# First feed-forward sums moved from GpSimd to VectorE, and operand splits issued piece by piece, in a one-layer decoder trunk

## The chip, the core and the metric

One NeuronCore of a Trainium2 chip runs the whole kernel. The metric is the device time of one launch in microseconds (us), given as the median of several runs. A difference is told as a share of the time before.

## The reference

One decoder layer (DEPTH = 1) on x of 2048 tokens by 1024 features, all in float32:

```
h = rmsnorm(x);  proj = h @ w_in                    # 1024 -> 4624
ya = conformer_mixer(...);  yb = gmlp_mixer(...);  yc = mamba2_mixer(...)
x = x + concat([ya, yb, yc]) @ w_out                # 2048 -> 1024
h = rmsnorm(x)
x = x + square(relu(h @ w_ff1)) @ w_ff2             # 1024 -> 4096 -> 1024
return rmsnorm(x)
```

## The kernel before

**Precision.** TensorE (PE) works on 32-bit operands that are split: `hi` is the operand cast to the engine's rounded 32-bit type (ScalarE, ACT), `lo` is the operand less `hi` (VectorE, DVE). Every product is three matmuls, hi*hi, lo*hi and hi*lo. Each operand is therefore a load into a raw tile (issued by SyncE, SP), a cast on ACT and a subtraction on DVE before PE can use it. A cast or a subtraction of a 128x512 tile is one instruction.

**Stages.** The tokens are worked on in two halves (h = 0, 1) of 1024.

- In-projection and the three mixers, up to 1012 us.
- Out-projection: four blocks, (h, kb), where kb = 0 and 1 are the two 1024-row halves of the contraction. A block has 4 column groups nq by 4 steps c0; a step is 48 matmuls of 128x256 (`mm3`, L243 to L245). PSUM is evicted to the accumulator by DVE (L1064 for kb = 0, L1074 for kb = 1); two tiles of PSUM turn round, so an eviction may be one step late before PE waits. The weights of the next nq are loaded and split by `load_wo`/`split_w` (L231 to L233), the left sides of the next block by `load_y`/`load_split` (`hi_y`, `lo_y`), both inside a scheduling priority (`evac`) that moves their instructions ahead.
- FF1 (first feed-forward layer): each half by a seven-product scheme (Strassen-Winograd), 16 pairs j by 7 products q, two pairs taken together, so 14 steps to a group and 224 steps in all. A step is 12 matmuls of 128x512 (L988 to L990). Its left sides are w1 blocks and their sums (`sum_w1`, L970 to L975, four 128x512 operations a pair, on GpSimd, POOL), its right sides the seven x operands of that half (`load_xi`, 4 pieces each, in L946 a load, in L927/L928 the splits). Four PSUM tiles are used for products 0 to 3 and 6 and four for 4 and 5.
- After FF1's products come the squared relu on ACT and, for the second layer's right sides, sums of the results: three on POOL (L1155 to L1157) and one on DVE (L1167), all stored to DRAM (`f_d`).
- FF2: the same seven products, 12 matmuls a step, right sides `fr` split into `fahi`/`falo`, left sides `wbhi`/`wblo`.

**Prepared sums.** `prep` makes 36 items (sums of blocks of the normalized input and of the second layer's weights, `PREP`) that go back to DRAM (`t_d`, `w2t_d`): a load of two pieces into one of two buffers `pr` (L912), four 128x256 operations on POOL (L920 to L923), a store (L924). Items are taken in the last block of the out-projection, one a step, and then a few for each group of FF1. FF1's x operands of q = 1, 3, 4 and 6 are read back from `t_d`.

**Order.** The program is written as one sequence, and a scheduler orders each engine's instructions by priority; each engine then runs its own in order, waiting on semaphores. `evac` raises a priority, `behind` ties an instruction behind another without a wait. Preparation of FF1 runs ahead of its products by fixed leads, in steps (`LEADW` 7 for w1 loads, `LEADS` 5 for sums, `LEAD1` 3 for splits, `LEADX` 9 for the second half's x operands), in `ahead1`; the first seven calls of it stand after the out-projection's last block. SP issues nearly all loads from one queue; POOL issues the stores of `f_d`'s sums, ACT of the others.

Of the kernel before, what the change touches and what calls it, by code (L numbers as in the profile page):

```python
# [41 lines left out]
def kernel(  # L42
# [179 lines left out]

    def split_w(pl, src, nk, ncol, tag, name, rk, bufs=2, rbufs=2, rpl=None):
# [14 lines left out]
    def mm3(pairs, n):  # L238


        for i, outs in enumerate(pairs):
# [673 lines left out]
    def prep_sum(key, after):  # L915
# [4 lines left out]
        behind(nc.gpsimd.tensor_sub(b11, b12, b11), after)  # L920
        nc.gpsimd.tensor_sub(b12, b22, b12)
        nc.gpsimd.tensor_sub(b22, b22, b11)
        nc.gpsimd.tensor_sub(b21, b21, b22)  # L923
# [8 lines left out]
    def load_xi(h, q):  # L932

        pl, bufs = (opnd, KT * NB) if q < 4 else (xb[0], 12)
        out_ = []
        for k in range(4):
            hi = pl.tile([P, 512], F32R, tag="hi", name=f"xhi_{h}_{q}_{k}", bufs=bufs)
            lo = pl.tile([P, 512], F32R, tag="lo", name=f"xlo_{h}_{q}_{k}", bufs=bufs)
            raw = const.tile([P, 512], F32, tag="raw", name=f"xr_{h}_{q}_{k}", bufs=RAWB)
            if q in TI:  # L940
                src = t_d[h][TI[q], k * P:(k + 1) * P, :]
            else:
                kk, th = {0: (k, 0), 2: (k + 4, 0), 5: (k + 4, 1)}[q]
                src = h2_d[h][kk * P:(kk + 1) * P, th * 512:th * 512 + 512]
            with evac() if h == 0 else contextlib.nullcontext():
                nc.sync.dma_start(raw, src)  # L946
                split_to(raw, hi, lo)
            out_.append((hi, lo))
        XS[h, q] = out_
# [13 lines left out]

    def sum_w1(h, j, q):
# [3 lines left out]
        if q == 1:  # L968
            w[3], w[1] = [ffa.tile([P, 4, P], F32, tag="s", name=f"ws{i}_{h}_{j}", bufs=4) for i in range(2)]
            nc.gpsimd.tensor_add(w[3], a21, a22)  # L970
            nc.gpsimd.tensor_sub(w[1], w[3], a11)
        elif q == 4:
            nc.gpsimd.tensor_sub(a21, a11, a21)
        elif q == 5:
            last["s4"] = nc.gpsimd.tensor_sub(w[1], a12, w[1])  # L975
            w[5] = w[1]

    def split_w1(h, j, q):
        hi = ffa.tile([P, 4, P], F32R, tag="hi", name=f"w1hi_{h}_{j}_{q}", bufs=5)
        lo = ffa.tile([P, 4, P], F32R, tag="lo", name=f"w1lo_{h}_{j}_{q}", bufs=5)  # L980
        split_to(WR[h, j][q], hi, lo)
# [30 lines left out]
    for bi, (h, kb) in enumerate(blocks):  # L1012
# [67 lines left out]
        preload(1)  # L1080
        ys = ynew
    prep(sums=True)

    GRP = 2
    LEADW, LEADS, LEAD1, LEADX, LEAD2, LEADB = 7, 5, 3, 9, 3, 16
    seq1 = [(h, g * GRP + i, q) for h in range(NHALF) for g in range(NPAIR // GRP) for q in range(NP)
            for i in range(GRP)]
# [298 lines left out]
```

## Time and profile before

| | |
|---|---|
| median of 3 runs | 2720.04 us (2716.86 to 2723.82) |
| profiled execution | 2722.77 us, span 2721.0 us |
| PE busy | 2650.2 us, 97% of the span |
| DVE, ACT, POOL busy | 63%, 49%, 34% |
| mean granted clock of PE | 0.992 of full speed |

Matmuls are pipelined, so a PE that is drawn busy may still run below its rate; the count of matmuls in a stretch, against the count in an equal stretch without waits, tells what was lost. Shares of busy time of the other engines are averages over stages: POOL's work lies mostly between 1446 and 2100 us.

### The profile page before, as it was taken

The numbers are of one execution on the slowest core, as the hardware profiler recorded it, in microseconds if no ns is written. First come the engines' busy times: TensorE is split into PE (matmuls) and PEld (weight loads), VectorE is DVE, ScalarE is ACT, GpSimd is POOL, SyncE is SP. The second block draws the span as 40 slices with busy tenths as digits, with TensorE's granted clock in tenths as the row PEclk, the third lists the DMA queues.
The fourth block names the chain that finished last, engine by engine and source line by source line (L and its number), as shares of the span: only waits on it lengthen the run. The fifth ranks groups of instructions, "written<-read, shape, count | busy, mean of one in ns | idle before, by whom it ended". The sixth has DMA issues, their size and how long they took to land. (4 is left out here: it accounts for less than half of the span.)

```text
span 2721.0 us, 38968 instructions
## 1 busy us (share of the span) xinstructions
PE 2650.2 (97%) x14018; PEld 2221.0 (82%) x14018; DVE 1710.5 (63%) x2289; ACT 1327.9 (49%) x2469; POOL 915.6 (34%) x980
## 2 busy tenths in 40 slices
PE   8999999999999999999998999989999999999998
PEld 6788887778878889999997788768887888888887
DVE  6778875596997844754436766886665434545434
ACT  5547673476686343543235455555444433333332
POOL 1013243123343221213054898687896000000001
PEclk9999999999999999999999999999999999999999
DMA  3343443334343236556478666676665645555543
GB/s 119 104 130 116 148 132 94 95 116 134 117 141 119 76 115 199 186 178 214 139 248 276 203 211 203 218 240 202 207 208 193 218 147 166 190 178 178 166 120 124
DMA packets 386897, 446.80 MB, mean 164 GB/s; under 512 B 28300, under 2 KB 279920, under 8 KB 386704
## 3 DMA queue, kind: packets, MB, share of 16 engines
q1 hardware_dynamic: 335520, 314.02, 38.0%
q0 software_dynamic: 28352, 96.62, 9.6%
q10 hardware_dynamic: 22832, 33.68, 3.5%
q8 instruction: 110, 1.80, 0.3%
q14 instruction: 83, 0.68, 0.1%
HBM read 297.28 MB, written 146.93 MB: 163 GB/s over the span
## 5 line engine op out<-in xcount | busy, mean ns | idle before, releaser
L988 PE MATMUL f<-xhi,w1hi 128*128 128x512 f32 x896 | 354.6, 396 | 18.2 <-DVE u L1138 12.1
L989 PE MATMUL f<-xlo,w1hi 128*128 128x512 f32 x896 | 353.9, 395 | 1.7 <-DVE xlo L928 1.7
L988 PE MATMUL f<-wbhi,fahi 128*128 128x512 f32 x896 | 349.4, 390 | 6.2 <-ACT wbhi L927 6.2
L990 PE MATMUL f<-xhi,w1lo 128*128 128x512 f32 x896 | 353.5, 395 | 1.3 <-DVE w1lo L928 1.3
L928 DVE TENSOR_TENSOR falo<-fr,fahi 128x512 fp32r<-128x512 f32 (+1 forms) x240 | 156.9, 655 | 314.2 <-ACT fahi L927 295.7
L989 PE MATMUL f<-wblo,fahi 128*128 128x512 f32 x896 | 349.2, 390 | 0.3 <-DVE wblo L928 0.3
L990 PE MATMUL f<-wbhi,falo 128*128 128x512 f32 x896 | 349.0, 390 | 0.0
L927 ACT CAST fahi<-fr 128x512 fp32r<-128x512 f32 (+1 forms) x240 | 141.8, 592 | 371.1 <-PE f L989 362.9
L530 DVE SCALAR_TENSOR_TENSOR ca<-ht,caw,ca 128x1024 f32<-128x1024 f32 x240 | 316.1, 1317 | 5.8 <-ACT ca L526 2.6
L243 PE MATMUL mmo<-whi_o,hi_y 128*128 128x256 f32 x1024 | 297.9, 291 | 16.8 <-DVE x L1074 9.6
L245 PE MATMUL mmo<-whi_o,lo_y 128*128 128x256 f32 x1024 | 291.4, 285 | 0.0
L244 PE MATMUL mmo<-wlo_o,hi_y 128*128 128x256 f32 x1024 | 291.1, 284 | 0.0
L988 PEld LDWEIGHTS f<-xhi,w1hi 128*128 128x128 f32 x896 | 169.7, 189 | 58.4 <-issue 8.1
L243 PEld LDWEIGHTS mmo<-whi_o,hi_y 128*128 128x128 f32 x1024 | 196.1, 191 | 20.6 <-DVE x L1074 10.7
L1260 POOL TENSOR_SCALAR ss<-ss 128x1 f32<-128x1 f32 x16 | 8.4, 522 | 592.6 <-ACT junk L1256 592.6
L989 PEld LDWEIGHTS f<-xlo,w1hi 128*128 128x128 f32 x896 | 169.9, 190 | 40.4 <-DVE xlo L928 2.6
L990 PEld LDWEIGHTS f<-xhi,w1lo 128*128 128x128 f32 x896 | 169.9, 190 | 40.2 <-DVE w1lo L928 2.1
L988 PEld LDWEIGHTS f<-wbhi,fahi 128*128 128x128 f32 x896 | 168.6, 188 | 41.6 <-ACT wbhi L927 6.7
L989 PEld LDWEIGHTS f<-wblo,fahi 128*128 128x128 f32 x896 | 168.6, 188 | 35.8 <-DVE wblo L928 0.8
L244 PEld LDWEIGHTS mmo<-wlo_o,hi_y 128*128 128x128 f32 x1024 | 196.2, 192 | 1.5 <-issue 1.4
L990 PEld LDWEIGHTS f<-wbhi,falo 128*128 128x128 f32 x896 | 168.6, 188 | 34.9
L245 PEld LDWEIGHTS mmo<-whi_o,lo_y 128*128 128x128 f32 x1024 | 195.8, 191 | 0.0
(299 smaller groups left out, 6031.4 us busy)
## 6 DMA issues: line engine op xcount, KB each, us to landing
fr<-f_d SPq DMA_DIRECT2D x208, 256.0 KB, 2.7
w<-in_w_ff_dram SPq DMA_DIRECT2D x176, 256.0 KB, 2.9
f_d<-fs POOLq DMA_DIRECT2D x96, 256.0 KB, 2.7
abc<-acs_d SPq DMA_DIRECT2D x32, 512.0 KB, 4.8
raw_y<-y_d SPq DMA_DIRECT2D x64, 256.0 KB, 4.0
wraw_o<-in_w_out_dram SPq DMA_DIRECT2D x64, 256.0 KB, 4.0
pr_w<-in_w_ff_dram SPq DMA_DIRECT2D x64, 256.0 KB, 4.8
w2t_d<-pr_w POOLq DMA_DIRECT2D x32, 512.0 KB, 4.4
```

The lines of the kernel that those rows point to most:

```text
L243: nc.tensor.matmul(ps, lh, rh, start=(i == 0 and j == 0), stop=False)
L244: nc.tensor.matmul(ps, lh, rl, start=False, stop=False)
L245: nc.tensor.matmul(ps, ll, rh, start=False, stop=(i == n - 1 and j == len(outs) - 1))
L530: nc.vector.scalar_tensor_tensor(acc, ht[:, k:k + T], caw[:, k * 4 + t:k * 4 + t + 1], acc, op0=ALU.mult, op1=ALU.add)
L927: nc.scalar.copy(hi, raw)
L928: nc.vector.tensor_sub(lo, raw, hi.bitcast(F32))
L988: nc.tensor.matmul(ps, lh, rh, start=start and i == 0, stop=False, skip_group_check=True)
L989: nc.tensor.matmul(ps, lh, rl, start=False, stop=False, skip_group_check=True)
L990: nc.tensor.matmul(ps, ll, rh, start=False, stop=last, skip_group_check=True)
L1260: nc.gpsimd.tensor_scalar(s_[:, 1:2], s_[:, 1:2], s_[:, 0:1], EPS, op0=ALU.add, op1=ALU.add)
```

## The change

- The w1 sums (4 for each of 32 pairs), the three POOL sums of FF1's results (32 times) and the four operations of prepared items from the 17th on go from POOL to DVE. Prepared items 0 to 15, those of the out-projection's last block, stay on POOL. All stores stay where they are.
- The out-projection's weights are loaded and split in pieces of 256 rows, one a step: piece z + 4 is split and piece z + 6 loaded at step z. The next block's left sides (`y_step`) and FF1's right sides (`x_step`) are loaded four at a time and split one call later, two a step in FF1.
- `pin` ties each of these casts and subtractions into program order on its engine; `early` does so for the w1 sums and splits ahead of step 0.
- The seven leading calls of `ahead1` stand in the last three steps of the out-projection.
- In FF2 the first three pairs of splits are pinned, w2 ahead of f.

```diff
+    def pin(ins):
+        return tc.keep_in_program_order(ins)
...
+    def raw_split(raw, name, g=None):
+        hi, lo = hi_lo(name)
+        if g is None:
+            pin(nc.scalar.copy(hi, raw))
+            pin(nc.vector.tensor_sub(lo, raw, hi.bitcast(F32)))
...
-            prep_sum(PREP[m], after)
+            prep_sum(PREP[m], after, nc.gpsimd if m < 16 else nc.vector)
...
-        behind(nc.gpsimd.tensor_sub(b11, b12, b11), after)
-        nc.gpsimd.tensor_sub(b12, b22, b12)
...
+        behind(eng.tensor_sub(b11, b12, b11), after)
+        eng.tensor_sub(b12, b22, b12)
...
+    def x_step(h, i, n=4):
+        for m in range(i - n, i):
+            if 0 <= m < 4 * NP:
...
+                raw = xraw.pop(0)
+                pin(nc.scalar.copy(hi, raw))
+                pin(nc.vector.tensor_sub(lo, raw, hi.bitcast(F32)))
+                XS.setdefault((h, q), []).append((hi, lo))
+        for m in range(i + 4 - n, i + 4) if i else range(4):
...
+                xraw.append(raw_load(src, f"x{h}_{q}_{k}"))
...
-            nc.gpsimd.tensor_add(w[3], a21, a22)
-            nc.gpsimd.tensor_sub(w[1], w[3], a11)
+            early(nc.vector.tensor_add(w[3], a21, a22))
+            early(nc.vector.tensor_sub(w[1], w[3], a11))
...
+    def wo_load(z):
+        if z < 4 * len(wo_seq):
+            h, kb, nq = wo_seq[z // 4]
+            r0 = kb * D + z % 4 * 256
+            raw = wor[z] = wp.tile([P, 2, NQ], F32, tag="wraw", name=f"wraw_o{z}", bufs=3)
...
             for c0 in range(0, NCH, 2):
-                if nq == 3 and c0 == 4:
-                    preload(0)
+                z = 16 * bi + 4 * nq + c0 // 2
+                wo_split(z + 4)
+                wo_load(z + 6)
+                if nq == 3 and c0 > 0:
+                    y_step(c0 // 2 - 1)
...
+                if bi == len(blocks) - 1 and nq == 3 and c0 > 0:
+                    for n in {2: (-7, -6), 4: (-5, -4, -3), 6: (-2, -1)}[c0]:
+                        at[0] = n
+                        ahead1(n)
...
-            nc.gpsimd.tensor_add(s1, f21, f22)
-            nc.gpsimd.tensor_sub(s2, s1, f11)
-            st[j, "s3w"] = nc.gpsimd.tensor_sub(f21, f11, f21)
+            nc.vector.tensor_add(s1, f21, f22)
+            nc.vector.tensor_sub(s2, s1, f11)
+            st[j, "s3w"] = nc.vector.tensor_sub(f21, f11, f21)
...
+        if n < 10:
+            x_step(0, 10 + 2 * n, 2)
+        i = n - (NP * NPAIR - LEADX)
+        if i == -2 or 0 <= i < 14:
+            x_step(1, max(0, 2 * i + 2), 2)
...
-    with tc.high_priority(offset=2000):
-        for u in range(LEAD2):
+    start2 = [True]
+    for u in range(LEAD2):
+        with tc.high_priority(offset=2000):
+            load_w2(u)
             load_f(u)
-            load_w2(u)
+    start2[0] = False
```

DVE near the end of FF1's first half, before the change: `u_0_14` is an eviction that frees a PSUM tile, `xlo_*` are splits of the second half's right sides, `w1lo` of the left sides.

```order
L1167 TENSOR_TENSOR fs_0_13_16292<-f_d_13_16288,fs_0_13_16236 128x512
L928 TENSOR_TENSOR w1lo_15_2_16339<-w_0_15_01_16125,w1hi_15_2_16338 128x512
L928 TENSOR_TENSOR xlo_0_0_16404<-xr_0_0_16405,xhi_0_0_16403 128x512
L928 TENSOR_TENSOR xlo_0_1_16410<-xr_0_1_16411,xhi_0_1_16409 128x512
L928 TENSOR_TENSOR xlo_0_2_16416<-xr_0_2_16417,xhi_0_2_16415 128x512
L928 TENSOR_TENSOR w1lo_14_3_16359<-ws_0_14_16210,w1hi_14_3_16358 128x512
L928 TENSOR_TENSOR xlo_0_3_16422<-xr_0_3_16423,xhi_0_3_16421 128x512
L1138 TENSOR_TENSOR u_0_14_16355<-p_0_14_16317,f_0_14_16342 128x512
```

The same eviction and the next one on DVE after the change; `ws` are sums of w1 blocks, `pr_w` a prepared item.

```order
L939 TENSOR_TENSOR pr_w_16156<-pr_w_16156 128x256
L940 TENSOR_TENSOR pr_w_16156<-pr_w_16156 128x256
L941 TENSOR_TENSOR pr_w_16156<-pr_w_16156 128x256
L942 TENSOR_TENSOR pr_w_16156<-pr_w_16156 128x256
L1202 TENSOR_TENSOR u_0_14_16355<-p_0_14_16317,f_0_14_16342 128x512
L1013 TENSOR_TENSOR w1lo_15_3_16387<-ws_0_15_16243,w1hi_15_3_16386 128x512
L1001 TENSOR_TENSOR ws_1_0_16634<-w_1_0_10_16478,w_1_0_11_16480 128x512
L1002 TENSOR_TENSOR ws_1_0_16635<-ws_1_0_16634,w_1_0_00_16474 128x512
L1004 TENSOR_TENSOR w_1_0_10_16478<-w_1_0_00_16474,w_1_0_10_16478 128x512
L1202 TENSOR_TENSOR u_0_15_16383<-p_0_15_16336,f_0_15_16370 128x512
L1013 TENSOR_TENSOR w1lo_14_4_16408<-w_0_14_10_16102,w1hi_14_4_16407 128x512
L964 TENSOR_TENSOR xlo_0_0_16412<-raw_x_0_0_16362,xhi_0_0_16411 128x512
```

The x splits stand behind both evictions now, and sums of w1 blocks and of a prepared item have come in ahead of and between them.

SP at the end of the out-projection and the start of FF1, before: `x_d` are stores of the out-projection's result, `pr_w` loads of prepared items, `xr_1` and `xr_2` loads of the right sides of FF1's second and third product.

```order
L839 DMA x_d_66<-x_1_0_3_11836 128x2x256
L912 DMA pr_w_13516<-in_w_ff_dram 128x2x256
L946 DMA xr_1_0_13494<-t_d_8401 128x512
L946 DMA xr_1_1_13500<-t_d_8401 128x512
L912 DMA pr_w_13516<-in_w_ff_dram 128x2x256
L946 DMA xr_1_2_13506<-t_d_8401 128x512
L946 DMA xr_1_3_13512<-t_d_8401 128x512
L946 DMA xr_2_0_13676<-h_d_67 128x512
L839 DMA x_d_66<-x_1_2_3_11838 128x2x256
```

The same stretch of SP after the change, where those loads are called `raw_x_1` and `raw_x_2`.

```order
L858 DMA x_d_66<-x_1_0_3_11820 128x2x256
L931 DMA pr_w_13516<-in_w_ff_dram 128x2x256 x2
L858 DMA x_d_66<-x_1_2_3_11822 128x2x256
L256 DMA raw_x_1_0_13508<-t_d_8401 128x512
L256 DMA raw_x_1_1_13510<-t_d_8401 128x512
L256 DMA raw_x_1_2_13512<-t_d_8401 128x512
L256 DMA raw_x_1_3_13514<-t_d_8401 128x512
L931 DMA pr_w_13627<-in_w_ff_dram 128x2x256 x2
L931 DMA pr_w_13754<-in_w_ff_dram 128x2x256 x2
L858 DMA x_d_66<-x_1_4_3_11824 128x2x256
L256 DMA raw_x_2_0_13619<-h_d_67 128x512
L256 DMA raw_x_2_1_13621<-h_d_67 128x512
```

The loads of the second product's right side now stand behind a second store of the result, those of the third behind two further prepared items.

ACT at the start of FF2, before: `f_d` is the last result of FF1, `fahi` and `wbhi` are casts of FF2's right and left sides.

```order
L1110 ACTIVATE f_d_15_19510<-u_1_15_19295 128x512
L1111 ACTIVATE f_d_15_19510<-f_d_15_19510 128x512
L1129 DMA f_d_8404<-f_d_15_19510 128x512
L927 CAST fahi_0_19528<-fr_0_19526 128x512
L927 CAST fahi_0_19540<-fr_0_19538 128x512
L927 CAST fahi_0_19552<-fr_0_19550 128x512
L927 CAST fahi_0_19571<-fr_0_19569 128x512
L927 CAST wbhi_0_19534<-w_0_0_00_19532 128x512
```

The same stretch after.

```order
L1174 ACTIVATE f_d_15_19510<-u_1_15_19295 128x512
L1175 ACTIVATE f_d_15_19510<-f_d_15_19510 128x512
L1193 DMA f_d_8404<-f_d_15_19510 128x512
L1284 CAST wbhi_0_19528<-w_0_0_00_19526 128x512
L1284 CAST fahi_0_19534<-fr_0_19532 128x512
L1284 CAST wbhi_1_19540<-w_0_1_00_19538 128x512
L1284 CAST fahi_0_19546<-fr_0_19544 128x512
```

The first cast of a left side has moved from behind four casts of right sides to the place right behind FF1's last result.

## Rows read from the trace of the kernel before

**Rows 1.** The page: busy time, share and instructions of each engine.

```profile
PE 2650.2 (97%) x14018; PEld 2221.0 (82%) x14018; DVE 1710.5 (63%) x2289; ACT 1327.9 (49%) x2469; POOL 915.6 (34%) x980
```

**Rows 2.** Stretches: length, busy time (instructions) of engines, clock, DMA share, GB/s.

```profile
1012.00:1121.00 109.00, 106.17 (x891) 103.24 (x890) 59.43 (x100) 50.46 (x112) 18.64 (x18) 0.98 0.60 191
1121.00:1233.00 112.00, 111.01 (x943) 107.68 (x942) 71.84 (x145) 57.89 (x160) 24.27 (x24) 1.00 0.62 200
1233.00:1337.00 104.00, 99.67 (x827) 99.46 (x826) 43.30 (x70) 30.46 (x58) 18.53 (x18) 0.98 0.50 159
1337.00:1446.00 109.00, 100.34 (x818) 99.49 (x817) 45.79 (x95) 38.65 (x111) 50.36 (x66) 0.97 0.78 249
1446.00:1512.00 66.00, 59.24 (x253) 46.83 (x251) 43.88 (x54) 37.38 (x71) 37.43 (x42) 0.97 0.76 249
1720.00:1810.00 90.00, 76.21 (x307) 60.68 (x306) 81.07 (x76) 48.05 (x86) 64.85 (x63) 0.92 0.73 243
1810.00:2090.00 280.00, 280.00 (x1221) 228.82 (x1220) 180.26 (x187) 141.20 (x231) 221.72 (x222) 1.00 0.60 199
2090.00:2110.00 20.00, 13.51 (x51) 10.28 (x50) 11.27 (x17) 10.59 (x19) 11.16 (x14) 0.83 0.73 254
2110.00:2712.00 602.00, 602.00 (x2657) 498.64 (x2657) 279.50 (x439) 216.74 (x408) 18.16 (x28) 1.00 0.53 166
```

**Rows 3.** Waits of PE: who was waited for, us in total, times, longest.

```profile
PE f L988 <- DVE u L1138: 12.1, 4, 5.6
PE mmo L243 <- DVE x L1074: 9.6, 5, 3.6
PE mmo L243 <- DVE x L1064: 7.2, 2, 4.3
PE f L988 <- ACT wbhi L927: 6.2, 1, 6.2
```

**Rows 4.** The page's DMA issues: transfers, size, us to landing.

```profile
wraw_o<-in_w_out_dram SPq DMA_DIRECT2D x64, 256.0 KB, 4.0
```

**Rows 5.** Waits of ACT from 1012 to 1520 us.

```profile
ACT w1hi L927 <- POOL ws L971: 19.2, 2, 12.4
```

**Rows 6.** Timeline of DVE in the last block: start, duration, what, idle before.

```profile
1396.72 0.81 DVE L233 TENSOR_TENSOR wlo_o<-wraw_o,whi_o 128x512 fp32r<-128x512 f32 x1 [6.63 <-ACT whi_o L232]
```

**Rows 7.** Waits of SP's queue from 1340 to 1480 us.

```profile
SPq L912 <- DMA w2t_d<-pr_w: 24.6, 8, 7.3
SPq L912 <- DMA t_d<-pr: 17.6, 4, 6.6
```

**Rows 8.** Loads of prepared weights, 1340 to 1480 us: shortest, median, longest ns; first and last start.

```profile
L912 SPq DMA_DIRECT2D pr_w<-in_w_ff_dram x20: 539/549/1091, 1390.5 to 1457.0; - x20
```

**Rows 9.** DVE's groups in FF1, 1520 to 2090 us: busy us, mean ns, idle before.

```profile
L928 DVE TENSOR_TENSOR w1lo<-w,w1hi 128x512 fp32r<-128x512 f32 x114 | 121.8, 1071 | 11.3 <-ACT w1hi L927 11.3
L1167 DVE TENSOR_TENSOR fs<-f_d,fs 128x512 f32<-128x512 f32 x28 | 45.7, 1632 | 41.6 <-POOL fs L1156 39.0 <-issue 2.6
L928 DVE TENSOR_TENSOR xlo<-xr,xhi 128x512 fp32r<-128x512 f32 x28 | 38.6, 1397 | 3.5 <-ACT xhi L927 3.5
```

**Rows 10.** DVE's largest group in FF2, 2120 to 2700 us.

```profile
L928 DVE TENSOR_TENSOR falo<-fr,fahi 128x512 fp32r<-128x512 f32 x199 | 137.5, 691 | 286.2 <-ACT fahi L927 267.9 <-PE f L989 14.2 <-DMA xin<-x_d 2.0
```

**Rows 11.** Timeline of DVE at the end of FF1's first half.

```profile
1735.17 0.68 DVE L928 TENSOR_TENSOR w1lo<-w,w1hi 128x512 fp32r<-128x512 f32 x1
1735.78 7.67 DVE L928 TENSOR_TENSOR xlo<-xr,xhi 128x512 fp32r<-128x512 f32 x3
...
1745.99 0.68 DVE L1138 TENSOR_TENSOR u<-p,f 128x512 f32<-128x512 f32 x1
```

**Rows 12.** Waits of SP's queue in FF1, 1440 to 2100 us.

```profile
SPq L959 <- DVE w1lo L928: 317.1, 91, 9.1
```

**Rows 13.** Timeline of ACT at the start of FF2.

```profile
2098.71 2.18 ACT L927 CAST fahi<-fr 128x512 fp32r<-128x512 f32 x4 [0.40 <-ACT f_d L1111]
2100.79 2.69 ACT L927 CAST wbhi<-w 128x512 fp32r<-128x512 f32 x5
```

More of the change, by code (lines that the diff above doesn't have):

```diff
@@ L248, in mm3, with raw_load @@
                 pump()
+    def raw_load(src, name):
+        raw = const.tile([P, 512], F32, tag="raw", name=f"raw_{name}", bufs=RAWB)
+        nc.sync.dma_start(raw, src)
+        return raw
+    def raw_split(raw, name, g=None):
[3 more added lines that the diff above has]
+            pin(nc.vector.tensor_sub(lo, raw, hi.bitcast(F32)))
+        else:
+            pin(nc.scalar.activation(hi, raw, AF.Copy, scale=g))
+            pin(nc.vector.scalar_tensor_tensor(lo, raw, g, hi.bitcast(F32), op0=ALU.mult, op1=ALU.subtract))
+        return hi, lo
     def load_split(src, name, g=None):
@@ L930 @@
     XS = {}
[L932 to L949, printed above, removed]
+    xraw = []
+    def x_step(h, i, n=4):
+        for m in range(i - n, i):
+            if 0 <= m < 4 * NP:
+                q, k = m // 4, m % 4
+                pl, bufs = (opnd, KT * NB) if q < 4 else (xb[0], 12)
+                hi = pl.tile([P, 512], F32R, tag="hi", name=f"xhi_{h}_{q}_{k}", bufs=bufs)
+                lo = pl.tile([P, 512], F32R, tag="lo", name=f"xlo_{h}_{q}_{k}", bufs=bufs)
+                raw = xraw.pop(0)
[3 more added lines that the diff above has]
+        for m in range(i + 4 - n, i + 4) if i else range(4):
+            if m < 4 * NP:
+                q, k = m // 4, m % 4
+                if q in TI:
+                    src = t_d[h][TI[q], k * P:(k + 1) * P, :]
+                else:
+                    kk, th = {0: (k, 0), 2: (k + 4, 0), 5: (k + 4, 1)}[q]
+                    src = h2_d[h][kk * P:(kk + 1) * P, th * 512:th * 512 + 512]
+                xraw.append(raw_load(src, f"x{h}_{q}_{k}"))
     WR, WS = {}, {}
@@ L991, in mm3c, with ahead1, wo_split @@
             clk.pe += 3 * 227.0
-    def load_wo(h, kb, nq):
-        return [split_w((wp, wo)[q], wout[kb * D + q * 512:kb * D + (q + 1) * 512, nq * NQ:(nq + 1) * NQ], 4, NQ, "w",
-                        f"o{h}{kb}{nq}{q}", 2, 2, 3, wp) for q in range(2)]
+    GRP = 2
+    LEADW, LEADS, LEAD1, LEADX, LEAD2, LEADB = 7, 5, 3, 9, 3, 16
+    seq1 = [(h, g * GRP + i, q) for h in range(NHALF) for g in range(NPAIR // GRP) for q in range(NP)
+            for i in range(GRP)]
+    bank, st = {}, {}
+    PG = (8, 10, 11, 13)
+    xb, fwp, ps4 = [], [], []
+    def ahead1(n):
+        for lead, f in ((LEADW, load_w1), (LEADS, sum_w1), (LEAD1, split_w1)):
+            if 0 <= n + lead < len(seq1):
+                h, j, q = seq1[n + lead]
+                if f is not load_w1:
+                    f(h, j, q)
+                elif q == 0:
+                    f(h, j)
+    WO, wor = {}, {}
+    def wo_load(z):
[3 more added lines that the diff above has]
+            raw = wor[z] = wp.tile([P, 2, NQ], F32, tag="wraw", name=f"wraw_o{z}", bufs=3)
+            nc.sync.dma_start(raw, wout[r0:r0 + 256, nq * NQ:(nq + 1) * NQ].rearrange("(k p) c -> p k c", p=P))
+    def wo_split(z):
+        if z < 4 * len(wo_seq):
+            q = z % 4 // 2
+            if z % 2 == 0:
+                WO[z // 2] = [(wp, wo)[q].tile([P, 4, NQ], F32R, tag="w" + t, name=f"w{t}_o{z}", bufs=2)
+                              for t in ("hi", "lo")]
+            hi, lo = (t[:, z % 2 * 2:z % 2 * 2 + 2, :] for t in WO[z // 2])
+            raw = wor.pop(z)
+            pin(nc.scalar.copy(hi, raw))
+            pin(nc.vector.tensor_sub(lo, raw, hi.bitcast(F32)))
     ys = ynext[0]
     blocks = [(h, kb) for h in range(NHALF) for kb in range(2)]
-    wq2 = [(h, kb, nq) for h, kb in blocks for nq in range(4)]
-    wn = load_wo(*wq2.pop(0))
+    wo_seq = [(h, kb, nq) for h, kb in blocks for nq in range(4)]
+    for z in range(4):
+        with evac():
+            wo_load(z)
+            wo_split(z)
+    wo_load(4)
+    wo_load(5)
     ys[1] = load_y(0, 0, 1)
-    accs = {}
+    accs, yraw, ycur = {}, [], None
     def load_x(h, nq):
@@ L1079 @@
                     spawn(gen_n2(h, c0, nq, acc), ("n", h))
[L1080 to L1081 removed]
+        ys, ycur = ynew, y_step
     prep(sums=True)
[L1084 to L1087, printed above, removed]
[L1088 to L1104 removed]
     def ftile(nm):
@@ L1168, in ff1 @@
             store(5, s4, nc.gpsimd)
-    for n in range(-LEADW, 0):
-        ahead1(n)
+    at[0] = 0
     xbs = ctx.enter_context(ExitStack())
```

66 lines of the change are left out of this document (32 added, 34 removed).

## The prediction

> **What bounds the kernel now.** I read the page's busy shares first. PE is busy for 2650 us, 97% of the span [rows 1], so other engines' work costs only where PE waits for it, and the whole prize is what PE loses. DVE at 63% and POOL at 34% are averages; the stages have to be taken apart.
>
> The view by stretches does that [rows 2]. In it the reader is to see, for each stretch, length, PE's count and the granted clock. Two undisturbed stretches give the rates: 1810 to 2090 us has 1221 matmuls in 280.0 us, 0.2293 us each, and FF2 (2110 to 2712) 2657 in 602.0, 0.2266. For the out-projection, block 1 (1121 to 1233) has 943 in 111.0 busy, 0.1177. Length less count times rate is the loss of each other stretch, idle time and slow clock together:
>
> - block 0: 109.0 - 891 x 0.1177 = 4.1 us
> - block 1: 1.0; block 2: 104.0 - 97.3 = 6.7
> - block 3: 109.0 - 96.3 = 12.7
> - start of FF1 (1446 to 1512): 66.0 - 253 x 0.2293 = 8.0
> - middle of FF1 (1720 to 1810): 90.0 - 70.4 = 19.6, with the clock at 0.92, between the levels of 1.2 and 2.4 GHz
> - start of FF2: 20.0 - 51 x 0.2266 = 8.4
>
> Together 60.5 us. A few matmul records may be missing, so each is good to about 1 us. The list of PE's waits, third, names who was late [rows 3]: the evictions L1064 and L1074 in the out-projection, u of L1138 in FF1, the cast wbhi in FF2. So the change can bring 60 us at most, whatever else it moves.
>
> **Out-projection, blocks 0 to 2.** The evictions were late because ACT and DVE, which run in order, stood behind something not yet there. In block 2 ACT waited 12.4 us for a w1 sum of POOL that the scheduler had drawn ahead into the out-projection [rows 5]; DVE's subtractions and an eviction stood behind it. The change writes the w1 preparation into the last three steps of block 3, and the pinned splits keep their place, so this wait has nothing left to happen to: I take 7.0 of the 7.7 us of blocks 1 and 2 (bounds 0 and 7.7). In block 0 the wait on late splits goes (up to 4.1), but the first pieces of the weights now turn round in three raw tiles: the fourth load waits for the first subtraction, and a load of that kind takes 4.0 us to land [rows 4], and two splitting operations of about 0.7 follow, 5.4 us against 4.3 us (36 matmuls) that PE has before it wants that piece; their casts also stand behind the last activation of the in-projection. A new wait of about 4 takes the old one's place: I take 0, with bounds of -5.4 and +4.1.
>
> **Block 3 and the start of FF1**, 12.7 + 8.0 = 20.7 us. In block 3 DVE stood 6.63 us behind a cast whose load was late [rows 6]; that load stood on SP behind loads of prepared items, which wait up to 7.3 us until a buffer has been stored [rows 7]. Loads of out-projection pieces are issued two steps (12 us) before their split now, which covers 7.3 + 4.0. What is late next is the chain of prepared items itself. It keeps POOL, as before, and two buffers: 10 items in 1390.5 to 1457.0 us, 7.4 us each [rows 8], against 96.3/16 = 6.0 us for a step of PE without waits. Over 16 items that chain lags by some 22 us less the lead it starts with, and the loads of FF1's second and third right sides stand behind it on SP (the second of the three pairs of orders shown). So the time won in block 3 is partly waited for in FF1's first ten steps. Bounds: nothing of the 20.7 (the chain paces both), or all of it. The chain's 7.4 us holds some waiting for PE's own evictions, by x_d's stores in the same queue, which gets shorter. I take the middle, 10.7.
>
> The stretch where this falls has 0.76 of the DMA engines busy and 249 GB/s [rows 2], among the highest of the stretches shown. The Trainium skill ("DMA: Bandwidth & Descriptors", section "Issuing engines are not separate DMA queues") says that transfers of all issuing engines run on the same 16 DMA engines and interleave; by it, finer loads in another order win nothing where those engines are full, and the term would be near its lower bound, 0. The row leaves a quarter of them free, so I do not go that far.
>
> **FF1.** POOL loses 352 operations (128 w1 sums, 96 sums of results, 128 of prepared items), DVE gets them. Their first effect is on DVE's other work. A DVE subtraction with both inputs in SBUF takes 691 ns in FF2, where POOL is idle [rows 10], but 1071, 1397 and 1632 ns for the three kinds in FF1 [rows 9]; at 1735.78 three of them took 7.67 us, and the eviction u behind them came at 1745.99 [rows 11], the longest wait of PE, 5.6 us [rows 3]. With POOL's tensor work gone from FF1 but for the items of block 3, they should take what they take in FF2.
>
> The second effect is load. For a group of 14 steps, 14 x 12 x 0.2293 = 38.5 us of PE, DVE gets for each of two pairs 5 evictions, 7 splits, 1 + 3 sums of results and 4 of w1, 40 operations, and 8 halves for two prepared items. An operation behind another costs 0.61 us (1735.17 to 1735.78) [rows 11]; for a half-width one I estimate 0.4. That is 40 x 0.61 + 8 x 0.4 = 27.6 us, 72% of the group: hidden. In the 14 steps before the second half, 28 splits of x come on top, 17.1 us, in all 44.7 in 38.5: a deficit of 6.2 us, against four PSUM tiles for each set of products, of which up to three steps (8.2 us) can wait. So between 0 and 6.2 of the 19.6 us stay; I take half, 3.1, and win 16.5. If the cover is gone, all 6.2 and the clock's share with it stay, and DVE in order decides (rival C).
>
> The Trainium skill ("VectorE: DVE Perf Modes", section "The DRAIN you can't avoid") says that a DVE operation starts only when the one before has left the pipeline. By that, 0.69 an operation, the 14 steps would hold 40 x 0.69 + 3.2 + 19.3 = 50.1 us, a deficit of 11.6, beyond the slack by 3.4, and the sum would be 3.4 less. The trace has a 0.68 us operation followed after 0.61, so the measured interval stands.
>
> **Start of FF2**, 8.4 us. ACT did four casts fahi (2098.71, 2.18 us) before the first wbhi at 2100.79 [rows 13]. In the new order wbhi stands first, fahi second: both are done two casts (1.1 us) after 2098.71, at 2099.8, against 2100.79 + 0.55 = 2101.3 before: 1.5 us. FF1's last sum on DVE is no longer stretched (1.63 to 0.69 [rows 9, 10]), 0.9, and the clock has less idle time to fall in, which I put at 0.6. 3.0 in all, bounds 1.5 and 8.4.
>
> **Sum.** 0 + 7.0 + 10.7 + 16.5 + 3.0 = 37.2 us. From the profiled execution's own 2722.8 us this gives 2685.6. That execution lies 2.7 above the median of the runs, so I expect about 2683 as a median.
>
> **The rivals.**
>
> A. The chain of prepared items paces block 3 and the start of FF1 together, so the 10.7 are given back as waits for right sides: 2683 + 10.7 = 2694. For it: SP's 24.6 and 17.6 us behind those items [rows 7]. Against it: the waits in block 3 were for other loads behind them.
>
> B. All waits go: 2720 - 60.5 = 2660. For it: each has a cause that the change touches. Against it: the first step of FF2 must wait for ACT after FF1's last result in any order.
>
> C. DVE at the change of halves is as late as before, since its new operations stand in order ahead of evictions: the 16.5 are not won, 2700. For it: the deficit of 6.2 us. Against it: single splits took more than three times 0.69.
>
> D. Slower: the w1 sums now wait on DVE, in order, for w1 loads, where on POOL nobody stood behind them but POOL. SP waits 317 us in FF1, 91 times, up to 9.1, until a w1 buffer is free [rows 12], so these loads leave as late as they can, two steps ahead of their sums. If DVE is held for more than 8.2 us by them in a group, PE waits for an eviction in each of 16 groups. At 3 us a group that is 48 us: 2720 - 20.7 (the terms outside the middle of FF1) + 48 = 2747. From 20.7/16 = 1.3 us a group on, the kernel is no faster. Against it: a load has 5.4 us and takes 4.0 to land by the nearest row [rows 4], so DVE would be held for about 1 us a group, within the slack.
>
> E. The change does not do what it says, because priorities put the instructions back where they were: no change, 2720. The order of instructions speaks against it, as 352 rows have left POOL and the evictions stand ahead of the x splits.
>
> **How the numbers follow.** Chances: the forecast 0.37, A 0.24, B 0.13, C 0.13, D 0.09, E 0.04. 0.3% of the time, 8.2 us, is what a measurement tells from no change; faster therefore means below 2712. All of the forecast, A, B and C lie below, 0.87; since a smaller form of D or of the wait in block 0 could take 10 to 20 us from them, I say 0.82 faster, 0.08 same, 0.10 slower. The range leaves out D and E and reaches from B to a little above C: 2658 to 2708.
>
> **What would show it.** Right: DVE's w1lo, xlo and fs groups at 0.68 to 0.75 us in FF1; no PE wait on u of L1138's successor near the change of halves above 3 us; L1064 and L1074 gone from PE's waits in blocks 1 to 3; in FF1's first ten steps waits for xhi, xlo or their evictions of 8 to 12 us; FF2's first matmul some 2.4 us nearer to FF1's last. A new wait for whi_o or wlo_o in block 0. Wrong: DVE idle behind DMA of w1 ahead of evictions in each group (D), a PE wait of 5 us and more for u at the change of halves (C), or FF1 starting as late against block 3's start as before (A).

## The result and the profile after

The changed kernel takes 2691.95 us (median of 4 runs, 2689.39 to 2694.75) against 2721.86 beside it, a ratio of 0.9893, 95% interval 0.9875 to 0.9911: 1.1% or some 29 us faster. The forecast was 2683 us, inside the range of 2658 to 2708; the time is nearer to rival A's 2694. The profiled execution took 2692.2 us (span 2690.5), 30.6 less than that of before.

The page's first part shows where the work went; it answers to [rows 1].

```profile
PE 2644.3 (98%) x14018; PEld 2216.7 (82%) x14018; DVE 1737.9 (65%) x2641; ACT 1326.1 (49%) x2469; POOL 499.9 (19%) x628
```

POOL lost 352 instructions and 416 us of busy time, DVE gained 352 and only 27 us: its own operations became shorter by nearly as much as the new ones cost. (The prepared items are 48 in all, by their 96 loads in the trace, and not 36; the last 32 moved, which makes 128 of the 352.) DVE's groups from 1490 to 2060 us (busy us, mean ns, idle before), against [rows 9]:

```profile
L1013 DVE TENSOR_TENSOR w1lo<-w,w1hi 128x512 fp32r<-128x512 f32 x118 | 80.5, 685 | 5.5 <-ACT w1hi L1012 5.5
L1231 DVE TENSOR_TENSOR fs<-f_d,fs 128x512 f32<-128x512 f32 x30 | 20.5, 683 | 0.0
L964 DVE TENSOR_TENSOR xlo<-raw_x,xhi 128x512 fp32r<-128x512 f32 x28 | 18.6, 686 | 2.8 <-ACT xhi L963 2.6
```

All three kinds are at FF2's figure now, as forecast. What PE waits for in the out-projection and behind it, against [rows 3] (us in total, times, longest):

```profile
PE f L1022 <- DVE w1lo L1013: 5.2, 3, 2.8
PE f L1021 <- DVE xlo L964: 4.4, 1, 4.4
PE f L1020 <- ACT fahi L1284: 3.9, 1, 3.9
PE mmo L247 <- ACT whi_o L1060: 3.7, 1, 3.7
PE f L1020 <- DVE u L1202: 2.1, 1, 2.1
PE mmo L247 <- DVE x L1161: 0.7, 1, 0.7
```

The evictions of the out-projection have gone from 16.8 us to 0.7, those of u from 12.1 to 2.1; new are whi_o at the start of the out-projection and splits at the start of FF1. In stretches (columns as in [rows 2]) these are the out-projection's third block, the start of FF1, and the two groups of 14 steps in which the right sides of the second half are split:

```profile
1239.00:1332.00 93.00, 92.95 (x776) 92.75 (x775) 34.91 (x59) 23.31 (x44) 7.76 (x10) 1.00 0.45 146
...
1431.00:1490.00 59.00, 49.59 (x201) 39.01 (x201) 43.25 (x80) 33.88 (x67) 7.91 (x10) 0.91 0.86 268
```

```profile
1733.00:1771.50 38.50, 38.28 (x167) 30.97 (x166) 33.62 (x57) 28.04 (x51) 5.12 (x9) 1.00 0.92 306
1771.50:1810.00 38.50, 38.50 (x169) 31.35 (x168) 35.69 (x65) 22.14 (x40) 6.65 (x11) 1.00 0.84 277
```

Block 2 has no idle time left. The start of FF1 has 9.4 us of it and a clock of 0.91: its first 14 steps take 54.0 us, 15.5 more than the 38.5 of a group without waits, so that some 6 us are lost beside the idle time, where the granted clock is lower than the 1.00 of block 2. In the change of halves DVE is busy for 69.3 of 77.0 us and PE for all but 0.2.

Some matmul records can be missing, so the stages are compared by the starts of their first and last matmuls in each profiled execution. Times are us; "first" is the start of the out-projection's first matmul, "2" and "3" are the last two blocks, "0-14" and "14-126" steps of FF1 (steps 98 to 126 hold the change of halves), "gap" lies between the last matmul of FF1 and the first of FF2. The ratio is to the kernel before in the same set of runs, and comparisons of two changed kernels are by these ratios; the stages are those of one execution each.

| kernel | median | ratio (95%) | first | 2 | 3 | 0-14 | 14-126 | gap |
|---|---|---|---|---|---|---|---|---|
| before | 2721.9 | 1 | 1012.6 | 98.6 | 109.9 | 46.4 | 332.3 | 6.6 |
| changed | 2692.0 | 0.9893 (0.9875-0.9911) | 1015.8 | 92.9 | 98.5 | 54.0 | 311.6 | 4.3 |
| 1 sums back on POOL | 2709.4 | 0.9964 (0.9952-0.9977) | 1017.8 | 92.0 | 99.4 | 53.4 | 328.7 | 5.1 |
| 2 sums alone | 2694.1 | 0.9913 (0.9897-0.9928) | 1013.2 | 95.8 | 108.2 | 42.8 | 311.2 | 5.9 |
| 3 12 items | 2677.8 | 0.9851 (0.9837-0.9864) | 1016.4 | 91.9 | 97.4 | 43.9 | 310.5 | 4.3 |
| 4 first splits free | 2687.2 | 0.9882 (0.9868-0.9895) | 1012.5 | 92.1 | 97.4 | 56.1 | 314.5 | 4.3 |
| 5 no ties | 2690.5 | 0.9902 (0.9885-0.9919) | 1012.7 | 98.8 | 104.6 | 43.9 | 310.1 | 5.9 |
| 6 w1 sums back | 2694.4 | 0.9913 (0.9898-0.9928) | 1016.6 | 91.9 | 98.8 | 53.0 | 312.7 | 4.3 |
| 7 = 3 + 4 | 2672.2 | 0.9831 (0.9817-0.9846) | 1013.0 | 92.0 | 98.7 | 42.1 | 311.5 | 4.3 |
| 8 = 7 + FF2 start | 2670.9 | 0.9827 (0.9812-0.9842) | 1012.5 | 91.9 | 98.9 | 41.7 | 313.1 | 0.2 |
| 9 items by POOL | 2725.4 | 1.0026 (1.0015-1.0036) | 1016.8 | 137.8 | 98.6 | 40.5 | 311.3 | 4.3 |
| 10 = 9 + 4 | 2718.5 | 1.0000 (0.9991-1.0009) | 1012.5 | 139.2 | 97.4 | 39.5 | 312.1 | 4.3 |
| 11 as 9, first 16 | 2694.4 | 0.9910 (0.9894-0.9926) | 1016.5 | 93.5 | 102.7 | 39.7 | 314.4 | 4.3 |
| 12 = 11 + 4 | 2686.4 | 0.9883 (0.9864-0.9902) | 1012.4 | 93.5 | 105.3 | 42.1 | 313.5 | 4.3 |

### The profile page after: what moved, and what is told of

Its sections match the earlier page's. It is cut to its first block, busy times and chain, and to the rows that moved or that the text cites. A ratio compares the mean times of both kernels' runs of the same rounds, so it can differ in the third digit from the quotient of the medians.

```text
span 2690.5 us, 38798 instructions
## 1 busy us (share of the span) xinstructions
PE 2644.3 (98%) x14018; PEld 2216.7 (82%) x14018; DVE 1737.9 (65%) x2641; ACT 1326.1 (49%) x2469; POOL 499.9 (19%) x628
## 4 chain that ended last, share of the span: by engine, by line
PE 84%; DVE 6%; DMA 3%; issue 3%; ACT 2%; POOL 2%; SPq 0%; ACTq 0%; DVEq 0%; POOLq 0%
PE f L1022 14%; PE f L1021 14%; PE f L1020 14%; PE mm L247 8%; PE mm L248 8%; PE mm L249 8%; PE mmo L247 4%; PE mmo L249 4%; PE mmo L248 4%; DVE ca L549 2%; PE yp L382 1%; DMA raw_x<-t_d 1%; PE sp L409 1%; PE op L372 1%; DVE cc L653 1%
## 5 line engine op out<-in xcount | busy, mean ns | idle before, releaser
L1022 PEld LDWEIGHTS f<-wbhi,falo 128*128 128x128 f32 x896 | 168.6, 188 | 35.5 <-DVE falo L1285 0.4
L247 PE MATMUL mm<-hi_h,whi_x 128*128 128x512 f32 x384 | 159.0, 414 | 0.0
```

Source lines behind the costliest of these rows:

```text
L247: nc.tensor.matmul(ps, lh, rh, start=(i == 0 and j == 0), stop=False)
L1022: nc.tensor.matmul(ps, ll, rh, start=False, stop=last, skip_group_check=True)
```

## The experiments

The theory after the result: POOL's tensor work stretched DVE and made the waits in the middle of FF1 (S); what the out-projection won was paid back at FF1's start, because the right sides' loads stand behind those of prepared items on SP (C, then H). The rivals are in the expectations.

**1. All 352 sums back on POOL.**

```diff
-            prep_sum(PREP[m], after, nc.gpsimd if m < 16 else nc.vector)
+            prep_sum(PREP[m], after, nc.gpsimd)
-            early(nc.vector.tensor_add(w[3], a21, a22))   # and the other six
+            early(nc.gpsimd.tensor_add(w[3], a21, a22))
```

> The changed kernel with all 352 sums back on POOL; pieces, ties and order of the splits stay. Theory S (POOL's tensor work stretches DVE's two-input operations, and that alone made the waits in the middle of FF1): w1lo and xlo take 1.0 us and more again in FF1, PE waits for u near the change of halves, and the time is 15 to 22 us above the changed kernel's 2692, about 2710. Rival P (the x splits of the second half, now issued two a step behind the evictions, made the gain there): at most 5 us above, 2692 to 2697, with no wait of PE for u over 2 us at the change of halves.

Measured: 0.9964, some 19 us above the changed kernel's ratio. Steps 14 to 126 are back at 328.7 us, though the x splits still stand two a step. PE's waits from 1700 to 1830 us, and three of DVE's groups from 1520 to 2050 us:

```profile
PE f L1022 <- DVE w1lo L1013: 11.1, 4, 5.7
```

```profile
L1013 DVE TENSOR_TENSOR w1lo<-w,w1hi 128x512 fp32r<-128x512 f32 x107 | 118.1, 1107 | 13.2 <-ACT w1hi L1012 13.2
L1013 DVE TENSOR_TENSOR w1lo<-ws,w1hi 128x512 fp32r<-128x512 f32 x80 | 106.5, 1332 | 14.3 <-ACT w1hi L1012 14.3
...
L1210 DVE TENSOR_TENSOR p<-p,f 128x512 f32<-128x512 f32 x54 | 37.0, 685 | 48.3 <-PE f L1022 48.3
```

S holds and P falls; the late operand is w1lo and no longer u, which S had wrong. The evictions `p`, which read one input from PSUM, keep their 685 ns, so DVE is not slower as such: only operations with both inputs in SBUF are.

The trace of the kernel before shows the same from one moment to the next. POOL made no sum from 1750.5 to 1771.1 us; DVE's splits just before, in and after that stretch:

```profile
1747.67 4.57 DVE L928 TENSOR_TENSOR xlo<-xr,xhi 128x512 fp32r<-128x512 f32 x3
...
1754.57 0.68 DVE L928 TENSOR_TENSOR xlo<-xr,xhi 128x512 fp32r<-128x512 f32 x1
...
1795.19 4.86 DVE L928 TENSOR_TENSOR xlo<-xr,xhi 128x512 fp32r<-128x512 f32 x2
```

```profile
1771.09 1.38 POOL L970 TENSOR_TENSOR ws<-w,w 128x512 f32<-128x512 f32 x1 [20.61 <-DMA w<-in_w_ff_dram]
```

Over that whole trace, the 174 splits w1lo and xlo beside which a POOL sum ran took 1426 ns on average, the other 106 took 684 and none more than 694. That POOL's sums were late, and not DVE's splits slow, is a rival that the waits rule out where PE lost its time: from 1520 to 2050 us ACT's casts waited 0.6 us for POOL in experiment 1. DVE itself waited 35.5 us there for POOL's sums of results, of which it needs one for `fs` (35.4 in the kernel before), but only 2.4 of them fell near the change of halves.

**2. The kernel before with the sums alone on DVE.** The edit is that of experiment 1 the other way, in the kernel before.

> The kernel before with only the 352 sums moved to DVE; all loads and splits in their old order. Theory S: the middle of FF1 is free of waits and FF2 starts a little sooner, the out-projection keeps its waits: 17 to 23 us below before, about 2702. Rival P: within 5 us of before's 2722, since three x splits in a row still stand ahead of an eviction. If POOL's w1 sums also made the out-projection's wait in block 2 (L971), that one goes too, and 6 more are won: about 2696.

Measured: 0.9913, 24 us, nearest to the expected case with a wait less in block 2, though that block gives only 2.8 of the 6 us (95.8 for 98.6). Steps 14 to 126 are at 311.2, with the x splits in their old order. The sums alone bring most of the whole change; the interval even overlaps that of the changed kernel, so that pieces, ties and order win anything in total is not shown. By the stages they do win 9.7 + 2.9 us in blocks 3 and 2, but step 14 of FF1 starts at 1485.9 us here and at 1485.3 in the changed kernel: what they win there is waited for again. The out-projection's waits are still there (1012 to 1446 us), against 16.8 us in [rows 3]:

```profile
PE mmo L243 <- DVE x L1074: 7.8, 4, 3.7
PE mmo L243 <- DVE x L1064: 6.3, 2, 3.2
```

**3. Twelve prepared items in the last block instead of sixteen.**

```diff
-                    prep(load=True, after=last["x1"])
+                    if prepq[0] < 12:
+                        prep(load=True, after=last["x1"])
...
-                prep(load=True, after=last["w1"])
+                prep(load=True, after=last["xr"] if n == 0 else last["w1"])
...
+            if n // (NP * GRP) in (0, 1):
+                prep(sums=True)
+        elif g == 1 and n // (NP * GRP) in (1, 2):
+            for _ in range(2):
+                prep(load=True, after=last["w1"])
```

Here `last["xr"]` is the newest load of a right side; the second and third group get one sum more at g == 6, and items from the 13th on are summed on DVE. So two things change at once: how many items stand ahead of FF1, and where its first two item loads stand on SP.

> The changed kernel with 12 instead of 16 prepared items in the out-projection's last block; the other four are made in groups 1 and 2 of FF1, and the first loads of items in FF1 stand behind the loads of the third product's right side and a few more. Theory C (the chain of prepared items on SP paces the first steps of FF1): the first 14 steps take 46 us or less instead of 54.0, SP's waits behind prepared items from 1330 to 1480 us fall from 50.7 to under 30 us, and the time is 6 to 10 us below the changed kernel, about 2684. Rival B (the right sides are late by their own loads and the DMA engines' share): the first 14 steps stay at 52 to 55 us, 2690 to 2694.

Measured: 0.9851, 11 us below the changed kernel; the first 14 steps take 43.9 us. SP's queue from 1330 to 1480 us, in the changed kernel and here:

```profile
SPq L931 <- DMA w2t_d<-pr_w: 34.8, 8, 6.9
SPq L931 <- DMA t_d<-pr: 15.9, 4, 6.4
```

```profile
SPq L933 <- DMA t_d<-pr: 14.5, 6, 3.3
SPq L933 <- DMA w2t_d<-pr_w: 7.7, 2, 4.2
```

The waits behind items fall from 50.7 to 22.2 us. That the chain of items on SP paced FF1's start is shown, by theory and rival as stated; which of the two changes did more is not. In the changed kernel's SP timeline the loads of the fourth and fifth right sides leave at 1447.75, right behind an item that waited, and ACT stands idle 5.01 us for them:

```profile
1445.80 1.21 SPq L931 DMA_DIRECT2D pr_w<-in_w_ff_dram  x2
1447.10 0.55 SPq L858 DMA_DIRECT2D x_d<-x  x1
1447.75 9.11 SPq L256 DMA_DIRECT2D raw_x<-t_d  x8
```

```profile
1452.58 1.91 ACT L963 CAST xhi<-raw_x 128x512 fp32r<-128x512 f32 x3 [5.01 <-DMA raw_x<-t_d]
```

**4. The first four weight splits free.**

```diff
-            pin(nc.scalar.copy(hi, raw))
+            tie = pin if z > 3 else (lambda ins: ins)
+            tie(nc.scalar.copy(hi, raw))
```

> The changed kernel with the first four splits of the out-projection's weights not tied into program order, so that the scheduler may put their casts ahead of the last activation of the in-projection. Theory T (the tie makes the wait of 3.7 us at the start of the out-projection): the first matmul of the out-projection starts 3 us sooner, and unless the fourth piece or the last left sides are late again by 4 us, the time is 2 to 6 us lower, about 2688. Rival L (the loads of the fourth piece and of the left sides decide): the wait moves to 1020 to 1025 us, 2690 to 2693.

Measured: 0.9882, 3 us below the changed kernel (intervals overlap). The wait for whi_o is gone, the first matmul starts 3.3 us sooner and block 0 takes 107.0 us for 109.0: T. (The same edit wins 7 us between experiments 9 and 10, whose intervals do not overlap.) In the changed kernel ACT's order shows the cause, zt of the last in-projection step ahead of the casts:

```profile
1014.67 0.59 ACT L755 ACTIVATE zt<-mm 128x512 f32<-128x512 f32 x1
1015.16 1.64 ACT L1060 CAST whi_o<-wraw_o 128x512 fp32r<-128x512 f32 x3
```

FF1 starts 7.0 us earlier, of which its first 14 steps (56.1) and the next (14 to 126, 314.5) give 5.0 back.

**5. No ties.** `pin` returns the instruction as it is.

> The changed kernel with the same pieces but no tie into program order; the scheduler alone orders the splits. Theory O (the ties keep ACT and DVE from standing behind loads that are late, so they made the out-projection's gain): the last two blocks of the out-projection, 92.9 and 98.5 us in the changed kernel against 98.6 and 109.9 before, get at least 5 of those 17 us back, and the time is 4 to 15 us above the changed kernel. Rival Z (loading and splitting in pieces is enough): within 3 us of the changed kernel, blocks within 2 us, or 3 below because the start of the out-projection comes sooner.

Measured: 0.9902, 2 us above the changed kernel, no difference that these runs can tell. By the total rival Z is right and theory O wrong, by the stages O is right: blocks 2 and 3 lose 12.0 us of their 17.1, and PE waits for evictions again (1000 to 1500 us):

```profile
PE mmo L247 <- DVE x L1151: 5.9, 2, 4.4
PE mmo L247 <- DVE x L1161: 5.6, 4, 2.6
```

The first 14 steps win 10.1 and the start 3.1, while the gap into FF2 grows from 4.3 to 5.9. It fits the chain that gains and losses cancel, since a later PE finds the items further on, but this run alone does not show it: the splits of FF1's first right sides lose their ties here too.

**6. Only the 128 w1 sums back on POOL.** The edit is the w1 part of experiment 1.

> The changed kernel with the 128 w1 sums alone back on POOL (the other 224 stay on DVE). With all 352 back, 93.7 us instead of 77.7 were taken by steps 98 to 126 of FF1. Theory S, in proportion: w1 sums are 44% of POOL's moved element work, so DVE's w1lo takes about 0.85 us, steps 98 to 126 take about 85 us, and the time is 5 to 10 us above the changed kernel. Rival T (DVE has room for some stretching, and only the whole of POOL's work went beyond it): steps 98 to 126 stay under 80 us and the time within 3 us. Rival W (these sums were slow on POOL, and the casts of w1 wait for them whoever else works): waits of ACT for POOL's ws, and the full 15 us or more.

Measured: 0.9913, 5 us above the changed kernel, but the intervals overlap, and in the profiled executions FF2 starts at the same time (2070.9 and 2071.0 us). Of w1lo, the splits of plain blocks take 865 ns and those of sums 700; xlo takes 804 (1396 in experiment 1); steps 98 to 126 take 81.3 us (77.7 and 93.7 in the changed kernel and experiment 1):

```profile
L1013 DVE TENSOR_TENSOR w1lo<-w,w1hi 128x512 fp32r<-128x512 f32 x108 | 93.2, 865 | 22.1 <-ACT w1hi L1012 22.1
L1013 DVE TENSOR_TENSOR w1lo<-ws,w1hi 128x512 fp32r<-128x512 f32 x84 | 58.8, 700 | 15.4 <-ACT w1hi L1012 15.4
...
L964 DVE TENSOR_TENSOR xlo<-raw_x,xhi 128x512 fp32r<-128x512 f32 x28 | 22.0, 804 | 3.4 <-ACT xhi L963 3.4
```

The expected 0.85 us comes for one group only; the splits of sums, 1332 ns in experiment 1, are almost back at the 685 of the changed kernel. Steps 98 to 126 lie between S (85 us) and T (under 80), and a cost in the total is not shown. W falls: ACT waits 2.1 us for `ws` from 1520 to 2050 us. So most of the 20 us came from the other 224 operations or from all of them together.

**7 and 8. Experiments 3 and 4 together; then ACT's path into FF2 shortened.** In 8 the last two pairs' squared relu, subtraction and stores are POOL's:

```diff
+                nc.gpsimd.tensor_scalar(f12, st[j, "u2"], 0.0, 0.0, op0=ALU.max, op1=ALU.add)
+                nc.gpsimd.tensor_mul(f12, f12, f12)
```

> Both edits that helped, together: 12 prepared items in the out-projection's last block, and the first four weight splits not tied. Alone they were worth some 11 and 2 us against the changed kernel, and the second one lost at the start of FF1 (first 14 steps 56.1 us instead of 54.0) what it had won. If the chain of items took it back, the sum is larger than the parts: first 14 steps at most 46 us, and 15 to 18 us below the changed kernel, about 2673. If the loss has another cause, 12 to 13 us, about 2677.

> As the kernel with both edits, and the squared relu of the last result of FF1's last two pairs is made on POOL, with its subtraction and store, so that ACT goes straight to the casts of FF2. If ACT's order alone makes the wait at the start of FF2 (4.3 us between the last matmul of FF1 and the first of FF2, and about 2.5 of slow clock behind it), the gap falls below 2 us and the time is 3 to 5 us below the kernel with both edits. If the tiles that these casts write come free only with FF1's last matmuls, the gap stays above 3 us and the time within 1.5 us.

Measured: 0.9831 for 7, 17 us below the changed kernel. That this is more than the parts (11 + 3) is less than these runs can tell, but the stages say the same: with a shorter chain the earlier start is kept, and the first 14 steps take 42.1 us, where experiment 4 had 56.1. It is faster than the kernel before and the changed kernel. For 8, 0.9827 (interval overlapping): the gap fell to 0.2 us as expected, but the time by 1.3 us only. PE now waits for the next splits, from 2040 to 2080 us:

```profile
PE f L1025 <- DVE falo L1303: 1.7, 1, 1.7
PE f L1024 <- DVE wblo L1303: 1.1, 1, 1.1
```

and steps 14 to 126 lost 1.6, which no edit there explains. That it is faster than 7 is not shown.

**9 and 10. The items' loads by POOL's queue.**

```diff
-            behind(nc.sync.dma_start(t[:, 2 * j:2 * j + 2, :],
+            eng = nc.gpsimd if prepq[0] < 18 else nc.sync
+            behind(eng.dma_start(t[:, 2 * j:2 * j + 2, :],
...
+                   after if prepq[0] >= 18 else None)
```

> The changed kernel with the loads of the first 18 prepared items issued by POOL's queue instead of SP's; the 16 items of the out-projection's last block stay there, with two buffers. It tells apart two readings of what fewer items in that block won. Theory H (the right sides' loads only stand behind the items' loads in SP's order): first 14 steps of FF1 at 42 to 46 us instead of 54.0, time about 11 us below the changed kernel, 2677. Rival V (the items' traffic and their DMA time slow the right sides, whatever queue issues them): first 14 steps at 50 us or more, time within 4 us of the changed kernel.

> The same, and the first four weight splits not tied. Theory H: 15 to 18 us below the changed kernel, about 2672, as with 12 items and free first splits. Rival V: the start of FF1 gives back what the start of the out-projection wins, 2685 to 2690.

Measured: 1.0026 and 1.0000; neither expectation came. The start of FF1 is at 40.5 and 39.5 us, but block 2 at 137.8 and 139.2. Untied, a sum of the 17th item stands early on DVE, ahead of evictions, and waits for its load (DVE, 1290 to 1365 us):

```profile
DVE pr_w L941 <- DMA pr_w<-in_w_ff_dram: 49.0, 1, 49.0
```

It is rival D's mechanism, made by this edit: DVE held in order by a load. PE reaches FF1 47 us later (at 1478.5 us, while the last of these loads left at 1358), so the short start does not decide between H and V.

**11 and 12. The same for the first 16 items only.** SP issues the loads from the 17th on, and all of them are tied behind other loads as in the changed kernel.

> As the kernel whose items are loaded by POOL's queue, but only the first 16 items' loads; from the 17th on SP issues them, behind the loads of the second right side, so that no sum of theirs on DVE can stand early in the out-projection (there DVE stood 49 us behind one). Theory H (right sides stand behind the items' loads in SP's order): the long wait in block 2 is gone (92 to 94 us), first 14 steps of FF1 at 40 to 45 us, time 9 to 14 us below the changed kernel, about 2678. Rival V (the items' work itself slows its neighbours, now in blocks 2 and 3, where POOL runs them as soon as their data is there): the blocks lose what FF1's start wins, within 4 us of the changed kernel's 2689 to 2692.

> The same, and the first four weight splits not tied. Theory H: about 2672, as the kernel with 12 items and free first splits; rival V: 2685 to 2690.

Measured: 0.9910 and 0.9883, within 5 us of the changed kernel: V by the total. H holds where it speaks of FF1's start (39.7 and 42.1 us), though a part of that can come from FF1's later start. But POOL runs the items earlier now, and in 11 FF1 starts 9.0 us later: block 3 takes 102.7 us for 98.5 (105.3 in 12), and there are new waits where blocks 2 and 3 begin. ACT waits longer for the left sides' loads from 1320 to 1440 us; changed kernel, 11, 12:

```profile
ACT hi_y L265 <- DMA raw_y<-y_d: 11.9, 6, 7.1
```

```profile
ACT hi_y L265 <- DMA raw_y<-y_d: 18.4, 9, 7.5
```

```profile
ACT hi_y L265 <- DMA raw_y<-y_d: 17.1, 7, 10.0
```

Why these loads are late is open. Their landings are known for one load in the changed kernel (3.2 us) and for two in each of the others, 5.9 and 6.5 in 11 but 2.6 and 2.5 in 12, whose block 3 is the longest; so that the items' transfers slow them is not shown. What is shown is that the items cost the start of FF1 by SP's order, and that moving them to POOL's queue brought no time in total; only taking some of them out of the out-projection (3, 7) paid.

## Why the prediction was right, and where not

By its steps, in us won in the profiled executions (differences of the table's rows):

| step | taken | measured |
|---|---|---|
| start of the out-projection and block 0 | 0 | -2.0 (first +3.2, block 110.2 to 109.0) |
| blocks 1 and 2 | 7.0 | 6.0 (113.2 to 112.9, 98.6 to 92.9) |
| block 3 and start of FF1 | 10.7 | 3.8 (11.4 - 7.6) |
| FF1 from step 14 | 16.5 | 20.7 |
| into FF2 | 3.0 | 2.3 |
| sum | 37.2 | 30.8 |

- **FF1.** Right in mechanism, and shown by 1 and 2 from both sides. The size was off, since I kept 3.1 us for a DVE deficit. In the two groups around the change of halves DVE has 122 operations and 69.3 us of work in 77.0: the x splits spread over more than the 14 steps (1733 to 1780 us), and no wait came of it (0.2 us). By the sentence of the Trainium skill that the prediction weighed ("VectorE: DVE Perf Modes", section "The DRAIN you can't avoid"), each operation would take its full time; I estimate 106 x 0.69 + 16 half-width ones x 0.42 (418 ns in the changed kernel's trace) = 80 us, which would not have fitted. But the same section goes on that a next operation that is not held starts earlier, which the prediction left out, and the trace agrees with that: 0.68 us operations start 0.61 apart [rows 11].
- **Block 3 and the start of FF1.** This is the step that failed in size: I took the middle between "the chain paces both" and "all is won", and the chain paced the two together. Block 3 won 11.4 and FF1's first 14 steps lost 7.6 of it, so 3.8 us were left of 10.7. I had counted on the chain's own waits getting shorter: its ten items behind 1384.1 us took 6.9 us each, for 7.4 [rows 8], still more than a step of PE. Experiments 3 and 7 win the missing part by moving four items. Rival A's mechanism was the right one. That its figure of 2694 is the nearest is in part luck: it gave this step nothing, and it took over the 2.7 us by which the profiled execution lay above the median, which was chance (0.2 us in the changed kernel).
- **Blocks 1 and 2.** Right. Half of block 2's 5.7 (2.8) comes with the sums alone [rows 5], by experiment 2; in the changed kernel all of it needs the ties, since without them block 2 takes 98.8 us again, by 5.
- **Block 0.** The expected new wait came (3.7 us for whi_o) and was dearer than the old by 2.0; its cause is the tie behind the in-projection's last activation, which the prediction named but did not price, by 4. The fourth load, which it priced at 5.4 us, is not what PE waited for.
- **Into FF2.** Right, and in its parts: with the sums alone (2) the gap is 5.9 us for 6.6, 0.7 for the shorter sum on DVE (0.9 taken), and without the ties (5), where four casts fahi stand ahead of wbhi again as in [rows 13], it is 5.9 for 4.3, 1.6 for the order (1.5 taken). What is left of the gap is ACT's path through the last squared relu, by 8.
- **Rival D.** DVE does wait in order for w1 loads, 22.5 us in 27 times, 2.7 at most, 1.4 us a group against the 1 I estimated, and PE's four tiles covered it. Experiments 9 and 10 show what it costs when the load is far away.

The errors had both signs (-2.0, -1.0, -6.9, +4.2, -0.7), so the sum was off by 6.4 us only, which is luck in part. The other 2.5 of the 9 us between forecast and median are the 2.7 taken off for the profiled execution, against 0.2 measured.

## What to carry to other kernels

Take an engine's work to another by the price it sets on its neighbours, not by its own load: POOL was 34% busy, and its sums cost PE 17 to 21 us in the middle of FF1 (experiments 1 and 2) through DVE's durations, while the 128 w1 sums by themselves cost next to nothing (6). Where two stages hang on one chain of small transfers in one queue, time won in the first shows up as a wait in the second until that chain is made shorter; sum the two stages before counting a gain. Tie splits into program order only where their operands are loaded early, and leave the first ones free; here the ties moved waits from one stage to another and in total won nothing that these runs can tell (5).

## What the runs showed of the hardware

- A DVE 128x512 subtraction with both inputs in SBUF (w1lo of plain blocks) took 685 ns without sums on POOL, 865 with 128 of them there and 1107 with all 352; evictions with one input in PSUM took 685 beside them too (experiment 1). The Trainium skill ("SBUF — State Buffer", section "Who interferes with whom") says that such an operation contends with a GpSimd one that reads SBUF; the three runs agree.
- One such subtraction can be held far longer than one POOL operation takes. In the kernel before this one took 8.16 us, while POOL ran eight sums of 0.7 to 1.3 us one behind the other:

```profile
1503.82 8.16 DVE L928 TENSOR_TENSOR w1lo<-ws,w1hi 128x512 fp32r<-128x512 f32 x1
```

- The prediction weighed that busy DMA engines leave finer loads in another order nothing to win (the Trainium skill, "DMA: Bandwidth & Descriptors", section "Issuing engines are not separate DMA queues", says that the transfers of all issuing engines share 16 DMA engines). The term did come out near its lower bound, but not for that reason: in experiment 7 the first 14 steps of FF1 took 42.1 us for 54.0 with the DMA engines busier, 0.88 against 0.83. The changed kernel, then experiment 7 (columns as in [rows 2]):

```profile
1431.30:1485.30 54.00, 44.59 (x178) 34.86 (x177) 39.84 (x74) 33.30 (x66) 6.81 (x8) 0.91 0.83 259
```

```profile
1424.90:1467.00 42.10, 40.93 (x179) 31.96 (x178) 35.59 (x67) 28.32 (x57) 1.51 (x2) 1.00 0.88 281
```
